# GLA and SSD of a hybrid mixer in three passes each: contributions, a walk over the states, outputs

## The chip, the cores and the metric

The kernel runs on one core of one Trainium2 chip. The metric is device time in microseconds for one execution of the whole program; where several runs are shown, it is their median. A time from the trace comes from one profiled execution.

## The reference

The program computes two layers of a mixer with four branches that share one input projection: RWKV-7, S5, SSD and GLA. A sequence has 256 context tokens and 1024 tokens of a grid, so 1280 columns in all; the model width is 1024 and each branch has 256 channels. Context and grid are separate sequences: the grid starts from the context's final state, and each branch runs in both directions. Layer 0 needs outputs of all 1280 tokens, layer 1 only of the 1024 (of the context it needs the states alone).

The two branches that matter here are chunked linear attentions. With d for the decay of a chunk, each keeps a state S for every head:

```
def chunk_state_pass(decay, contrib, s0):
    def step(S, inp):
        dec, ctb = inp
        return dec * S + ctb, S
    s_fin, prev = lax.scan(step, s0, (moveaxis(decay, 1, 0), moveaxis(contrib, 1, 0)))
    return moveaxis(prev, 0, 1), s_fin
# GLA: chunks of 64 tokens, 4 heads, 32 keys and 64 values a head, a decay for each key
contrib = einsum('bcqhk,bcqhv->bchkv', k * exp(b_last - bc), v)
y = einsum('bchij,bcjhv->bcihv', scores, v) + einsum('bcihk,bchkv->bcihv', q * exp(bc), prev)
# SSD: chunks of 128 tokens, 4 heads in 2 groups, 64 states, a decay for each head
contrib = einsum('bcqhn,bcqhp->bchnp', k * exp(cs_last - cs)[..., None], v)
y = einsum('bchij,bcjhp->bcihp', scores, v) + einsum('bcihn,bchnp->bcihp', q * exp(cs)[..., None], prev)
```

The outputs of both directions are added; then come a norm, a gate and, at the end of the layer, the output projection over all four branches.

## The kernel before

The program goes through each layer in three stages: the projection stage (`project`), the RWKV and S5 stage (`rw`) and the output projection (`out_proj`). GLA and SSD belong to the projection stage. Inside it the program order is: the projections of `misc` and `gk`, the preparation of S5, GLA with its projections, SSD with its projections, then the projections of RWKV and the rest. The framework schedules the instructions of all engines by a list: it takes program order as priority and a model of durations, so work that stands early in the program goes ahead where it is ready, and projections fill the rest of PE. The order of each engine is fixed at build time; on the chip each engine takes its queue in order and waits on semaphores.

Projections (`proj`, `proj_tok`, the tile `pj` in PSUM) multiply a split of each weight, `i_wh` and `i_wl`, made by ACT (L1550) and VectorE (L1551) from a load `i_w`, with a split of the normed input, `hi` and `lo`. Their results go through DRAM. All matmuls of the helper `mm` carry L320, all two-input elementwise operations L332, all activations L329, so the tiles tell them apart.

**GLA** (`gla`, L389). `qe` and `ke` are the scaled queries and keys of the two directions, features on the partitions (four heads of 32). The loop of L451 has 20 steps; a step handles one chunk of 64 forward and one backward (`ch`). In every second step two 128-column pieces of `ke` are transposed (`g_kp`), and in the first half of the loop `gla_pair` (L513) is called for the pair of chunks `j`: masked queries `g_qb`, scores in PSUM, mask (`g_P`), sum of both directions (`g_pa`), four matmuls with the values `V` (tile `l_gv`), and an ACT copy into `g_Y`. From step 1 on, two matmuls of 256 columns multiply `qe` by the state `g_S` (L472), and two VectorE operations add the result to `g_Y` (L476). Then eight small matmuls give the contributions of the step (L483), and VectorE adds them to the running state `g_Sd` (L488), spreads it over four heads by a mask into `g_S` (L491) and multiplies by the decay (L493). In layer 1 the outputs of the first four steps are left out.

**SSD** (`ssd`, L538). After a convolution (`s_cv`) and transposes (`s_xt`, `s_Bt`), the loop of L610 has 10 steps, one chunk of 128 forward and one backward. `ssd_pair` (L664) makes the part inside a chunk. The output term multiplies C (`s_x`) by the state `s_S` (L618), scales on VectorE (`s_yt`, L623) and adds on POOL (L625). Contributions come from weighted values `s_xw` made on POOL (L632) and matmuls with `s_Bt` (L635); VectorE updates the state `s_Sc` (L643, L644); ACT copies it into `s_S` (L648), whose zero blocks keep the groups apart.

Both end with a norm and a gate and with `y_out` (L374), which transposes the result on PE (L381, `ps<-con,s_Y`), scales on ACT and stores to DRAM. The large SBUF tiles of the stage (`T`) share eight buffers, the 2 KB tiles (`Q`) eleven. PSUM has the tags `pc` (2 buffers: states and contributions), `ps` (3), `pz` (1) and `pj` (2).

The RWKV stage starts with memsets, loads `r_in` and prepares its first blocks (`ps<-r_in`, a scan `r_cs`, `r_BK`, `r_AD`); its first large matmul is `pb<-r_AD,r_BK`.

Of the kernel before, what the change touches and what calls it, by code (L numbers as in the profile page):

```python
# [15 lines left out]
OP = mybir.AluOpType  # L16
# [238 lines left out]
class K:  # L255
# [133 lines left out]
    def gla(self, src, outs):  # L389
# [20 lines left out]
        gall, gs = self.S("gall", [128, 2, 20, 4]), self.S("g_gs", [128, 2, 20])  # L410
        k, q = src["gk"], src["gq"]
        for d in range(2):
# [19 lines left out]
            if d == 0:  # L432
                self.tt(g[:, 0:19], l3[:, 0:19], em[:, 1:20], OP.mult)
                nc.vector.tensor_copy(g[:, 19:20], l3[:, 19:20])
            else:
                self.tt(g[:, 0:3], l3[:, 3:0:-1], em[:, 2::-1], OP.mult)
                self.tt(g[:, 3:4], l3[:, 0:1], em[:, 19:20], OP.mult)
                self.tt(g[:, 4:19], l3[:, 19:4:-1], em[:, 18:3:-1], OP.mult)
                nc.vector.tensor_copy(g[:, 19:20], l3[:, 4:5])
            self.tt(gall[:, d], g.unsqueeze(2).to_broadcast([128, 20, 4]),  # L440
                    c("bm4").unsqueeze(1).to_broadcast([128, 20, 4]), OP.mult)
# [7 lines left out]
        Y = [self.T("g_Y", [128, 5, 256]) for _ in range(2)]  # L449
        St = Sp = None  # L450
        for s in range(20):  # L451
            ch = [s, 3 - s if s < 4 else 23 - s]
            jb = [x // 2 for x in ch]
            if s % 2 == 0:

                kp = next(kring)
                ps = self.P()
                for d in range(2):
                    nc.tensor.transpose(ps[:, d * 128:(d + 1) * 128], ke[d][:, jb[d] * 128:(jb[d] + 1) * 128], c("ident"))
                p3 = ps[:, :256].rearrange("p (a b) -> p a b", a=2)  # L460
                nc.scalar.copy(kp[0:64, :, 0, :], p3[0:64])
                nc.vector.tensor_copy(kp[64:128, :, 1, :], p3[64:128])
                first = s == 0 if s < 4 else s < 12
                if first and (outs or s >= 4):
                    for j in (jb if jb[0] != jb[1] else jb[:1]):
                        self.gla_pair(j, qe, ke, next(pring), V, Y)
            if s > 0 and (outs or s >= 4):

                ps = self.P("pc")[:, :256]
                for d in range(2):  # L470
                    r = 64 * (ch[d] % 2)
                    self.mm(ps[r:r + 64], qe[d][:, ch[d] * 64:(ch[d] + 1) * 64], St[:, d, :])  # L472
                for d in range(2):
                    j, r = jb[d], 64 * (ch[d] % 2)
                    y = Y[j // 5][r:r + 64, j % 5, :]
                    self.tt(y, ps[r:r + 64], y, OP.add)  # L476
            if s == 19:
                break
            ps = self.P("pc")[:, :128]
            for d in range(2):  # L480
                j, r = jb[d], ch[d] % 2
                for h in range(4):
                    self.mm(ps[32 * h:32 * h + 32, d * 64:(d + 1) * 64], kp[:, d, r, 32 * h:32 * h + 32], V[j // 5][:, j % 5, h * 64:(h + 1) * 64])  # L483

            cur = ps.rearrange("p (d v) -> p d v", d=2)
            Sd = self.S("g_Sd", [128, 2, 64], bufs=2)
            if Sp is not None:
                self.tt(Sd, cur, Sp, OP.add)  # L488
                cur = Sd
            Sn = self.Q("g_S", [128, 2, 256])  # L490
            self.tt(Sn.rearrange("p d (h v) -> p d h v", h=4), cur.unsqueeze(2).to_broadcast([128, 2, 4, 64]),  # L491
                    gall[:, :, s, :].unsqueeze(3).to_broadcast([128, 2, 4, 64]), OP.mult)
            self.tt(Sd, cur, gs[:, :, s:s + 1].to_broadcast([128, 2, 64]), OP.mult)  # L493
            Sp = Sd
            St = Sn
# [17 lines left out]
    def gla_pair(self, j, qe, ke, pa, V, Y):  # L513

        nc, c = self.nc, self.c
        pm = []
        halves = [slice(0, 64), slice(64, 128)]
        for d in range(2):
            qb = self.Q("g_qb", [128, 4, 128])
            self.tt(qb, qe[d][:, j * 128:(j + 1) * 128].unsqueeze(1).to_broadcast([128, 4, 128]),  # L520
                    c("bm4").unsqueeze(2).to_broadcast([128, 4, 128]), OP.mult, "p")
            ps = self.P()[:, :256]
            for h in halves:
                self.mm(ps[h], ke[d][:, j * 128 + h.start:j * 128 + h.stop], qb[:, :, h])
# [7 lines left out]
        ps = self.P()  # L532
        for h in range(4):
            self.mm(ps[:, h * 64:(h + 1) * 64], pa[:, h, :], V[j // 5][:, j % 5, h * 64:(h + 1) * 64])
        nc.scalar.copy(Y[j // 5][:, j % 5, :], ps[:, :256])  # L535


    def ssd(self, src, outs):  # L538
# [60 lines left out]
        Y = [self.T("s_Y", [128, 5, 256]) for _ in range(2)]  # L599
        cring = self.ring("s_cp", [128, 2, 128], 2)  # L600
        sring = self.ring("s_S", [128, 2, 256], 2)
# [7 lines left out]
        St = Sp = None  # L609
        for s in range(10):  # L610
            tl = [s, 1 - s if s < 2 else 11 - s]
            if (s == 0 or 2 <= s < 6) and (outs or s >= 2):
                for j in tl:
                    self.ssd_pair(j, B, C, next(cring), xt, stri, lap, dt, Y)
            if s > 0 and (outs or s >= 2):
                ps = self.P("pc")
                for d in range(2):
# [1201 lines left out]
```

## Time and profile before

| | us |
|---|---|
| median of 3 runs | 2274.1 |
| lowest and highest | 2272.3, 2274.61 |
| the profiled execution | 2271.75 |
| its span, first to last instruction | 2269.9 |

| engine | busy us | share of the span |
|---|---|---|
| PE (matmul) | 1970.1 | 87% |
| PEld (weight load) | 1652.5 | 73% |
| VectorE (DVE) | 1571.7 | 69% |
| ACT | 922.1 | 41% |
| POOL | 834.8 | 37% |

Busy shares are averages over the stages. By the stretches in which they run, the projection stage lies at about 0 to 669 us (layer 0) and 1290 to 1733 us (layer 1), the RWKV stage after each, the output projection last. PE's busy time counts matmuls from start to their modelled end; overlapping ones are counted once. The granted clock is the share of TensorE's full rate in a stretch. The waits of an engine name what ended an idle time.

### The profile page before, as it was taken

How to read it: one execution, taken by the hardware profiler on the slowest of the kernel's cores; microseconds unless marked ns; L12 is line 12 of the kernel's file. 1: busy time of each engine (PE TensorE's matmuls, PEld its weight loads, DVE VectorE, ACT ScalarE, POOL GpSimd, SP SyncE). 2: the span in 40 equal slices, each digit the busy share in tenths (PEclk: the TensorE clock that was granted, in tenths of full speed). 3: DMA queues.
4: the chain of work that ended last, by engine and by line, in shares of the span. 5: the costliest groups of instructions: out<-in, count | busy, mean ns of one | idle time of the engine just before them, and what ended most of it. 6: DMA issues, size and time to landing. Idle time of an engine off the chain costs nothing. (4 is left out here: it accounts for less than half of the span.)

```text
span 2269.9 us, 44142 instructions
## 1 busy us (share of the span) xinstructions
PE 1970.1 (87%) x17173; PEld 1652.5 (73%) x17176; DVE 1571.7 (69%) x3513; ACT 922.1 (41%) x2005; POOL 834.8 (37%) x947
## 2 busy tenths in 40 slices
PE   7797999999985888888998989999996678787897
PEld 5677788777774777766997777877885567676697
DVE  3876535866638987887477887368563898778654
ACT  3335212244436547544233552123452655564420
POOL 1446431113345535442322266301234355444222
PEclk9899999999997888898999899999998778797998
DMA  8134413454342323214333254234222232220532
GB/s 272 53 117 154 136 58 124 137 180 126 113 130 98 97 68 102 78 36 152 116 108 121 92 175 137 71 105 131 82 75 83 96 94 78 76 71 29 174 110 94
DMA packets 208049, 246.76 MB, mean 109 GB/s; under 512 B 28384, under 2 KB 150240, under 8 KB 207840
## 3 DMA queue, kind: packets, MB, share of 16 engines
q1 hardware_dynamic: 174832, 215.49, 30.4%
q10 hardware_dynamic: 33008, 28.45, 3.8%
q8 instruction: 135, 2.21, 0.4%
q14 instruction: 74, 0.61, 0.1%
HBM read 169.27 MB, written 76.71 MB: 108 GB/s over the span
## 5 line engine op out<-in xcount | busy, mean ns | idle before, releaser
L320 PE MATMUL pj<-hi,i_wh 128*128 128x512 f32 (+1 forms) x952 | 248.4, 381 | 19.2 <-DVE hi L1527 10.8
L320 PE MATMUL pj<-hi,i_wl 128*128 128x512 f32 (+1 forms) x952 | 247.4, 373 | 0.3 <-DVE i_wl L332 0.3
L320 PE MATMUL pj<-lo,i_wh 128*128 128x512 f32 (+1 forms) x952 | 245.9, 375 | 0.0
L320 PEld LDWEIGHTS pj<-hi,i_wh 128*128 128x128 f32 x952 | 169.4, 196 | 54.9 <-DVE hi L1527 11.3
L320 PEld LDWEIGHTS pj<-lo,i_wh 128*128 128x128 f32 x952 | 170.1, 195 | 35.1 <-issue 4.6
L320 PEld LDWEIGHTS pj<-hi,i_wl 128*128 128x128 f32 x952 | 166.6, 192 | 34.4 <-issue 5.0
L332 DVE TENSOR_TENSOR i_wl<-i_w,i_wh 128x512 fp32r<-128x512 f32 x108 | 86.3, 807 | 70.2 <-ACT i_wh L1550 34.4
L1550 ACT CAST i_wh<-i_w 128x512 fp32r<-128x512 f32 x108 | 66.3, 620 | 162.8 <-PE pj L320 127.3
L320 PE MATMUL pb<-r_AD,r_BK 128*128 128x256 f32 x320 | 98.3, 457 | 33.3 <-DVE r_BK L332 14.9
L320 PE MATMUL px<-r_UV,r_A 128*64 128x64 f32 x1216 | 109.4, 248 | 18.8 <-DVE r_UV L1378 9.5
L320 PEld LDWEIGHTS px<-r_UV,r_A 128*64 128x64 f32 x1216 | 93.5, 158 | 41.3 <-DVE r_UV L1378 13.5
L320 PEld LDWEIGHTS pb<-r_AD,r_BK 128*128 128x128 f32 x320 | 70.1, 231 | 47.8 <-POOL r_BK L332 22.8
L1288 DVE TENSOR_TENSOR r_X<-r_X,r_tp 128x30 f32<-128x30 f32 (+1 forms) x300 | 93.2, 311 | 7.7
L332 DVE TENSOR_TENSOR r_tp<-r_N,r_X 128x30 f32<-128x30 f32 (+1 forms) x300 | 91.4, 305 | 7.1
L332 DVE TENSOR_TENSOR g_Y<-pc,g_Y 64x256 f32<-64x256 f32 x70 | 29.4, 421 | 77.1 <-ACT g_Y L535 56.2
L332 POOL TENSOR_TENSOR r_S<-r_S,r_PM 64x256 f32<-64x256 f32 x72 | 54.7, 760 | 72.0 <-DVE r_S L332 66.8
L320 PE MATMUL pj<-i_wh,hi 128*128 128x256 f32 x448 | 71.6, 297 | 9.9 <-ACT i_o L329 5.0
L335 POOL TENSOR_SCALAR r_AD<-r_AR 64x512 f32<-64x512 f32 (+1 forms) x80 | 54.7, 684 | 50.9 <-PE pb L320 34.7
L320 PEld LDWEIGHTS pj<-i_wh,hi 128*128 128x128 f32 x448 | 61.9, 199 | 14.2 <-ACT i_wh L1550 5.6
L329 ACT ACTIVATE r_BK<-r_BK,r_PM 128x128 f32<-128x128 f32 x160 | 58.2, 399 | 31.7 <-PE pb L320 30.6
L332 POOL TENSOR_TENSOR s_Y<-s_Y,s_yt 128x256 f32<-128x256 f32 x34 | 29.1, 868 | 111.0 <-DVE s_Y L332 62.3
L320 PE MATMUL ps<-r_in,rconm 128*128 128x128 f32 x320 | 52.2, 312 | 19.5 <-ACT r_yt L1421 7.7
(466 smaller groups left out, 5156.1 us busy)
## 6 DMA issues: line engine op xcount, KB each, us to landing
i_w<-in_win SPq DMA_DIRECT2D x108, 256.0 KB, 3.0
r_in<-rm SPq DMA_DIRECT2D x36, 512.0 KB, 4.2
a_w<-in_ada SPq DMA_DIRECT2D x64, 256.0 KB, 3.2
rm<-i_o SPq DMA_DIRECT2D x48, 256.0 KB, 2.7
o_y<-yd SPq DMA_DIRECT2D x36, 256.0 KB, 3.2
i_o<-in_ada SPq DMA_DIRECT2D x32, 256.0 KB, 5.2
z_st<-s5t SPq DMA_DIRECT2D x32, 256.0 KB, 2.8
o_w<-in_wout SPq DMA_DIRECT2D x32, 256.0 KB, 2.9
```

Of the source, the lines that this page charges most:

```text
L320: self.nc.tensor.matmul(out, lhsT, rhs, start=start, stop=stop, skip_group_check=True)
L329: self.nc.scalar.activation(out=out, in_=in_, func=f, **kw)
L332: (self.nc.vector if e == "v" else self.nc.gpsimd).tensor_tensor(out, a, b, op)
L335: (self.nc.vector if e == "v" else self.nc.gpsimd).tensor_scalar(out, a, s1, s2, op0, op1)
L1288: last = nc.vector.tensor_tensor(X[:, :, :i, r0:4], X[:, :, :i, r0:4], tmp[:, :, :i, r0:], OP.add)
L1550: self.nc.scalar.copy(hi[:, v], w)
```

## The change

GLA: the loop of 20 steps becomes three passes. The first goes over the ten pieces of 128 columns: transposes, `g_kp`, sixteen small matmuls for the contributions of both chunks and directions into one PSUM tile, and two copies (VectorE for the forward, ACT for the backward direction) into the SBUF tiles `g_St`, ordered by step. The second is a walk over the 19 states in place: add the state before, multiply by the decay. The third calls `gla_pair` for each pair; it now adds the output of the states into the same PSUM bank as the part inside the chunk, by up to sixteen matmuls that take the masked queries `g_qb` as weights and 64 columns of a state. One ACT copy then writes the result over the values `V`. The spreading of the state over heads, its mask `gall`, `g_S` and the VectorE additions into `g_Y` are gone.

SSD: contributions of all ten chunks first, with copies into `s_St`; a walk of eight steps on VectorE (multiply, add); then for each chunk `ssd_pair` and the output term, whose matmuls now take the masked C (`s_cp`) of one group and 128 columns of a state, two for each direction. Both directions are scaled by one VectorE operation where both exist. The result overwrites the values `s_xt`.

```
@@ gla
-        Y = [self.T("g_Y", [128, 5, 256]) for _ in range(2)]
-        St = Sp = None
-        for s in range(20):
-            ...
+        St = [self.T("g_St", [128, 10, 2, 64]) for _ in range(2)]
+        step = lambda d, ch: ch if d == 0 else 3 - ch if ch < 4 else 23 - ch
+        for j in range(10):
+            ps = self.P()[:, :256]
             for d in range(2):
+                nc.tensor.transpose(ps[:, d * 128:(d + 1) * 128], ke[d][:, j * 128:(j + 1) * 128], c("ident"))
+            kp = next(kring)
+            ...
+            ps = self.P("pc")[:, :256].rearrange("p (d r v) -> p d r v", d=2, r=2)
+            for d in range(2):
                 for h in range(4):
-                    self.mm(ps[32 * h:32 * h + 32, d * 64:(d + 1) * 64], kp[:, d, r, 32 * h:32 * h + 32], V[j // 5][:, j % 5, h * 64:(h + 1) * 64])
-            ...
+                    for r in range(2):
+                        self.mm(ps[32 * h:32 * h + 32, d, r], kp[:, d, r, 32 * h:32 * h + 32], V[j // 5][:, j % 5, h * 64:(h + 1) * 64])
+            for d in range(2):
+                a = step(d, 2 * j)
+                ...
+                (nc.scalar.copy if d else nc.vector.tensor_copy)(o, ps[:, d])
+        for t in range(19):
+            o = St[t // 10][:, t % 10]
+            if t:
+                self.tt(o, o, St[(t - 1) // 10][:, (t - 1) % 10], OP.add)
+            self.tt(o, o, gs[:, :, t:t + 1].to_broadcast([128, 2, 64]), OP.mult)
+        Y = V
+        for j in range(0 if outs else 2, 10):
+            self.gla_pair(j, qe, ke, next(pring), Y, St, step)
@@ gla_pair
-        ps = self.P()
+        ps = self.P("pc")
+        y = Y[j // 5][:, j % 5]
         for h in range(4):
-            self.mm(ps[:, h * 64:(h + 1) * 64], pa[:, h, :], V[j // 5][:, j % 5, h * 64:(h + 1) * 64])
-        nc.scalar.copy(Y[j // 5][:, j % 5, :], ps[:, :256])
+            self.mm(ps[:, h * 64:(h + 1) * 64], pa[:, h, :], y[:, h * 64:(h + 1) * 64], h == 0, False)
+        for d in range(2):
+            for r in range(2):
+                ch = 2 * j + r
+                t = step(d, ch) - 1
+                if t >= 0:
+                    for h in range(4):
+                        self.mm(ps[64 * r:64 * r + 64, h * 64:(h + 1) * 64], qb[d][:, h, 64 * r:64 * r + 64], St[t // 10][:, t % 10, d], False, d == 1)
+        nc.scalar.copy(y, ps[:, :256])
@@ ssd
-        Y = [self.T("s_Y", [128, 5, 256]) for _ in range(2)]
+        Y = xt
-        sring = self.ring("s_S", [128, 2, 256], 2)
-        St = Sp = None
-        for s in range(10):
-            ...
+        St = [self.T("s_St", [128, 5, 2, 2, 64]) for _ in range(2)]
+        for j in range(10):
             ps = self.P("pc")
             xw = self.Q("s_xw", [128, 2, 4, 64])
             ...
+            for d in range(2):
+                t = step(d, j)
+                (nc.scalar.copy if d else nc.vector.tensor_copy)(St[t // 5][:, t % 5, d].rearrange("p h v -> p (h v)"), ps[:, d * 128:(d + 1) * 128])
+        for t in range(1, 9):
+            o, i = [St[u // 5][:, u % 5] for u in (t, t - 1)]
+            m = self.S("s_Sm", [128, 2, 2, 64], bufs=2)
+            self.tt(m, i, dc[:, :, t].unsqueeze(3).to_broadcast([128, 2, 2, 64]), OP.mult)
+            self.tt(o, o, m, OP.add)
+        for j in jobs:
+            cp = next(cring)
+            self.ssd_pair(j, B, C, cp, xt, stri, lap, dt, Y)
+            ds = [d for d in range(2) if step(d, j) > 0]
+            ps = self.P("pc")
+            for d in ds:
+                for g in range(2):
+                    self.mm(ps[:, d * 256 + g * 128:d * 256 + g * 128 + 128], cp[:, g], St[(step(d, j) - 1) // 5][:, (step(d, j) - 1) % 5, d].rearrange("p h v -> p (h v)"))
+            yt = self.Q("s_yt", [128, 2, 4, 64])
+            ...
```

## Rows read from the trace of the kernel before

**Rows 1.** Stretches: length, busy PE, PEld, DVE, ACT, POOL (count), PE clock, DMA.

```profile
250.00:418.00 168.00, 167.09 (x1381) 131.99 (x1380) 82.98 (x211) 33.54 (x67) 39.62 (x55) 0.99 0.33 104
...
519.00:655.00 136.00, 136.00 (x917) 104.59 (x916) 77.74 (x161) 53.18 (x123) 43.26 (x54) 1.00 0.37 110
...
669.50:686.70 17.20, 5.63 (x46) 5.02 (x45) 9.31 (x16) 10.59 (x22) 10.97 (x19) 0.80 0.86 279
1366.00:1530.00 164.00, 157.55 (x1232) 123.91 (x1230) 97.82 (x223) 37.07 (x77) 53.76 (x62) 0.97 0.32 101
...
1605.00:1733.50 128.50, 128.50 (x682) 105.52 (x682) 70.48 (x140) 54.58 (x123) 41.29 (x48) 1.00 0.24 69
1733.50:1768.20 34.70, 11.21 (x60) 9.51 (x61) 19.43 (x36) 11.96 (x26) 19.96 (x25) 0.62 0.36 109
```

**Rows 2.** Timeline of PE, end of layer 0's projections: start, length, operation, count [idle].

```profile
667.50 1.10 PE L320 MATMUL pj<-lo,i_wh 128*128 128x512 f32 x4
668.43 1.09 PE L320 MATMUL pj<-hi,i_wl 128*128 128x512 f32 x4
670.29 0.77 PE L381 MATMUL ps<-con,s_Y 128*128 128x128 f32 x5 [0.77 <-DVE s_Y L332]
...
686.66 3.73 PE L320 MATMUL pb<-r_AD,r_BK 128*128 128x256 f32 x8 [7.80 <-DVE r_BK L332]
```

**Rows 3.** Timeline of PE, end of layer 1's projections.

```profile
1732.39 1.10 PE L320 MATMUL pj<-hi,i_wl 128*128 128x512 f32 x4
1733.42 0.66 PE L320 MATMUL pc<-s_xw,s_Bt 128*64 128x128 f32 x8
...
1760.90 0.87 PE L381 MATMUL ps<-con,s_Y 128*128 128x128 f32 x3 [17.95 <-DVE qst L338]
...
1768.24 2.19 PE L320 MATMUL pb<-r_AD,r_BK 128*128 128x256 f32 x8
```

**Rows 4.** Timelines of DVE and POOL in the same place.

```profile
1736.76 0.76 DVE L332 TENSOR_TENSOR s_yt<-pc,s_ex 128x256 f32<-128x256 f32 x2 [2.21 <-PE pc L320]
...
1751.14 3.74 POOL L332 TENSOR_TENSOR s_sq<-s_Y 128x768 f32<-128x768 f32 x2
...
1762.27 1.49 DVE L332 TENSOR_TENSOR s_Y<-s_Y,qsy 128x1280 f32<-128x1280 f32 x1
```

**Rows 5.** Groups over the whole span: operation, count | busy us, mean ns | idle before.

```profile
L320 PE MATMUL px<-r_UV,r_A 128*64 128x64 f32 x1216 | 109.4, 248 | 18.8 <-DVE r_UV L1378 9.5 <-ACT r_UV L1347 7.7 <-POOL r_UV L1348 1.1
...
L320 PE MATMUL ps<-r_in,rconm 128*128 128x128 f32 x320 | 52.2, 312 | 19.5 <-ACT r_yt L1421 7.7 <-ACT r_a L329 6.9 <-DVE r_yt L338 4.8
...
L332 DVE TENSOR_TENSOR g_Y<-pc,g_Y 64x256 f32<-64x256 f32 x70 | 29.4, 421 | 77.1 <-ACT g_Y L535 56.2 <-PE pc L320 19.9
...
L332 DVE TENSOR_TENSOR g_S<-g_Sd,gall 128x512 f32<-128x512 f32 x36 | 28.9, 804 | 1.2
...
L320 PE MATMUL pc<-g_S,g_e 128*64 128x256 f32 x140 | 24.7, 410 | 0.7 <-DVE g_S L332 0.7
...
L320 PE MATMUL pc<-l_gv,g_kp 128*32 128x64 f32 x608 | 19.4, 228 | 0.4 <-DVE g_Y L332 0.4
...
L320 PE MATMUL pc<-s_S,s_x 128*128 128x256 f32 x68 | 18.8, 387 | 1.4 <-ACT s_S L648 1.4
...
L320 PE MATMUL pc<-s_xw,s_Bt 128*64 128x128 f32 x144 | 13.6, 290 | 0.0
```

**Rows 6.** Timeline of PE: one run of narrow RWKV matmuls and what follows.

```profile
1812.00 2.08 PE L320 MATMUL px<-r_UV,r_A 128*64 128x64 f32 x32
1814.01 0.75 PE L320 MATMUL pi<-r_DN,r_Am 32*32 32x32 f32 x64
```

**Rows 7.** Waits of PE from 1340 to 1734 us: total, times, longest.

```profile
PE pj L320 <- DVE i_o L338: 5.3, 8, 1.4
```

**Rows 8.** Timelines of SP and DVE where layer 1's GLA loop ends.

```profile
1529.52 0.33 SPq L1639 DMA_DIRECT2D l_sB<-f_sB  x1
...
1529.97 0.42 DVE L332 TENSOR_TENSOR g_Y<-pc,g_Y 64x256 f32<-64x256 f32 x1
```

## What the change will do, predicted before its result was known

> **What bounds the kernel now.** I read the busy time by stretch first, then the projection stage of each layer alone, then the two places where that stage hands over to the RWKV stage. GLA and SSD run inside the projection stage, beside the big projection matmuls, so the question is which engine is never free there. In the stretch of the GLA loop of layer 0 PE is busy 167.09 of 168 us, VectorE 82.98 and ACT 33.54; in the stretch of the SSD loop PE is busy 136.00 of 136; in layer 1 it is 157.55 of 164 and 128.50 of 128.5, at a granted clock of 0.97 to 1.00, that is the 2.4 GHz level nearly throughout [rows 1]. So while projections are left, PE work is the time, and VectorE has half of its time free: what the change saves on VectorE is worth little there by itself.
>
> Then come the two hand-overs. In layer 0 the last projection matmuls start at 668.43, the first big RWKV matmul (pb) at 686.66 [rows 2]; of that stretch of 17.2 us PE works 5.63 [rows 1]. In layer 1 the last projections start at 1732.39, but pb only at 1768.24 [rows 3]: 34.7 us with 11.21 busy, and the clock falls to 0.62 [rows 1]. The difference is the SSD of layer 1: its last output term (s_yt) is made at 1736.76, after the last projection; POOL squares at 1751.14; VectorE scales the result at 1762.27 [rows 4]; and PE, which takes its queue in order, stands 17.95 us before the transposes of s_Y at 1760.90 with pb queued behind them [rows 3]. In layer 0 the same transposes cost it 0.77 us [rows 2].
>
> **The change part by part.** Its time is counted against the profiled execution: 2271.75 us, 1.85 above its span of 2269.9; the median of the three runs, 2274.1, lies 2.35 higher, and I carry the difference over to the median.
>
> 1. GLA outputs on PE. Before, each step multiplies qe by the state St, spread to four heads: two matmuls of 64 output rows by 256 columns. A float32 matmul stands in the trace as two instructions, so the 19 + 16 steps make the 140 of the group, busy 24.7 us, 176 ns each [rows 5]. Now each pair of chunks makes up to sixteen matmuls of 64 columns, one for each direction, chunk and head: 152 in layer 0, 128 in layer 1, so 560 instructions. The nearest row is the RWKV matmul with the same shapes (128x64 weights, 64 columns): over the whole kernel 109.4 us for 1216, 90 ns each with all ends [rows 5]; in one unbroken run 32 of them take from 1812.00 to 1814.01, 63 ns each [rows 6]. A pair's sixteen are such a run of 32, so I take 63: 35.2 us, 10.5 more than now. The upper end is 90 ns: 50.4, 25.7 more. The lower end is below nothing: the present pairs lie in different halves of the output rows, and that two column groups can overlap is seen at the contributions, 608 instructions in 19.4 us or 32 ns each [rows 5]; if the two halves overlapped fully in the new order too, 35.2 would become 17.6, 7.1 less than now.
>
> Here a rule of the Trainium skill speaks against part of my price. The rows show 63 ns for narrow matmuls that follow one another in one half, and 32 ns where four column groups take turns [rows 5, 6]. The Trainium skill, "TensorE: Matmul & The Clock Gate", section "Part 3: Packing small matmuls — row/col tiling", says that matmuls in different column groups run at once but start strictly in program order. The new order does four in one half before the other half, so by that rule only the last of each four overlaps with its successor. What it would make is a rival below.
>
> 2. GLA contributions: 152 matmuls a layer become 160 (both directions of all ten pairs), 608 instructions become 640. At the present 32 ns that is 1.0 us more [rows 5], and I take it. The order is new: two chunks of one head, in one group of 32 rows, before the next head. The lower end is 0; the upper end, with no overlap left at all, is 63 ns, 20.9 more.
>
> 3. SSD outputs: 34 matmuls of 256 columns (68 instructions, 18.8 us) become 68 of 128 columns. The nearest row is the 128x128 by 128 matmul of the RWKV inputs, 52.2 us for 320 or 163 ns [rows 5]: 136 of these are 22.2, 3.4 more, which I take. Ends: 0 if it goes by columns alone, 18.7 if each costs 276 ns as the wide ones do.
>
> 4. SSD contributions: 36 a layer become 40, at 13.6 us for 144 instructions [rows 5]: 1.5 more.
>
> 5. Turns of PE. Four projection matmuls take 0.93 us when the next ones follow (667.50 to 668.43) and 1.03 when GLA or SSD work follows (1732.39 to 1733.42) [rows 2, 3]: a turn costs 0.1. GLA turned for 19 + 16 outputs and 38 contributions; it now turns 20 times for contributions, and the outputs go with the pair's last matmuls. 53 turns fewer are 5.3 us; many already shared a visit, so I take 3 (ends 0 and 5.3).
>
> PE's sum: 10.5 + 1.0 + 3.4 + 1.5 - 3 = 13.4 us more, and since PE is full it lies on the path.
>
> 6. VectorE, ACT and POOL. Gone are the spreading of the state to four heads (28.9 us) and the additions into g_Y (29.4) [rows 5], with ACT's copies of the SSD state; new are 40 copies of contributions out of PSUM on each of VectorE and ACT; the walk has as many small operations as the loop had. Some 45 us of VectorE are saved, all under PE's cover: I count the work at nothing. If that cover were gone it would be worth at most what PE now loses to VectorE there: the projections' waits for i_o are 5.3 us in layer 1 [rows 7]. I take 2 back. Either way is possible, since the convolution of SSD moves up beside those i_o operations, and i_o and the weight splits are queued behind each VectorE wait of the new pass: 5 gained to 5 lost.
>
> 7. Chains. In the GLA of before, output, addition and state share two PSUM buffers with the contributions of the next steps; the loop takes 164 us in layer 1 [rows 1]. SSD's loads start when it ends: sB is fetched at 1529.52 as the last g_Y is added at 1529.97 [rows 8]. In SSD each step goes PE, VectorE, ACT, PE, and each PE visit stands behind projections, so it ends at 1736.76 [rows 4]. Now both walks stay on VectorE, and the outputs of different pairs don't depend on each other. The added waits are: the walk for the last contribution, all outputs for the walk, and SSD's x times D on POOL for the four matmuls that read x (it now overwrites it; POOL's s_sg of the next pair is queued behind). None is for PE's projections. SSD need end only some 35 us earlier than now for its transposes, and the POOL and VectorE work before them, to lie under projections. Then the hand-over of layer 1 is like that of layer 0: 34.7 - 17.2 = 17.5 us less [rows 1]. What comes last then is the RWKV preparation itself (r_in, its scan, r_BK), which layer 0 shows. In layer 0 the 0.77 us go [rows 2]; I count 1 (0 to 3). No DMA is added; loads of SSD and the final stores move to earlier, where SP and ACT's queue have room.
>
> The sum: 13.4 - 17.5 - 1 - 2 = -7.1 us: 2264.6 for the profiled execution, **2267 us** for the median.
>
> **The rivals.** (a) The order rule above: of each four matmuls three run alone and the fourth beside the next, so 27.5 us instead of 35.2 (estimate from the 63 ns), PE +5.7 and the sum -14.8: 2259. For it speaks that one-group runs and taking turns differ in the rows as it says. Chance 0.20. (b) Both halves overlap fully, since the four instructions of a GLA step do so now: outputs -7.1, PE -4.2, sum -24.7: 2249. Against it: half of the order is in one group. Chance 0.13. (c) Slower: narrow matmuls cost 90 ns because sixteen in a row don't hide their weight loads, in both GLA loops, where nothing covers PE: PE +28.6, sum +8.1: 2282. It decides from 75 ns an instruction on, where the outputs' 42 us eat all that the hand-over gives. Against it: the unbroken run at 63. Chance 0.12. (d) Slower too: the hand-over stays, because all pairs of SSD are now queued after its walk and the last still ends after the last projection: 13.4 - 2 = +11.4: 2285. For it: pairs use the same three PSUM buffers as before; against it: the serial steps are gone from both loops. Chance 0.12.
>
> **How the numbers follow.** The forecast's own case has 0.35, from 2258 to 2275; 0.08 is left for shifts of order that I can't place, both ways. A measurement of this kernel tells about 0.2%, 4.5 us, from no change: faster is below 2269.6, slower above 2278.6. Faster: 0.23 of the forecast's case, all of (a) and (b), 0.02: 0.58. Slower: (d), 0.08 of (c), which reaches below the bound, and 0.03 of the rest: 0.23. Same: 0.12 of the forecast's case, 0.04 of (c) and 0.03 of the rest: 0.19. The range goes from 2242, below (b), to 2288, above (d). All upper ends of 1 to 3 at once would be 2315; I give that less than 0.05 and leave it out.
>
> **What would show it.** Right: the g_St matmuls at about 63 ns in runs of 32, some 35 us in all; the projections of layer 1 ending 5 to 10 us later after the stage's start than now; s_Y's transposes ahead of the last projections; pb within 18 us of them in both layers; PE still full between. Wrong: idle time of PE beside the walk; s_Y's transposes still last in layer 1; a price of narrow matmuls far from 63 ns; or a projection stage whose length doesn't follow PE's sum.

## The result: 30 us less, with the profile after

The changed kernel takes **2244.4 us** (median of four runs, 2239.62 to 2248.43) against 2274.36 us (four runs, 2272.3 to 2277.87) for the kernel before: ratio 0.9866, 95% interval 0.9843 to 0.9889. The profiled execution takes 2239.62 us with a span of 2237.8, 32.1 us under the 2269.9 of before. It was forecast to be faster, at 2267 within 2242 to 2288; the gain is four times the forecast one. The profiled execution is the quickest of the four. One of the six executions of rotate_c below took 5761 us and is left out of its median.

The two traces are cut at the same landmarks: first and last projection matmul of a layer, first big RWKV matmul (pb), first output projection. So the stretches are, in order: projection stage, hand-over and RWKV stage of layer 0; output projection of layer 0 with the projection stage of layer 1, hand-over and RWKV stage of layer 1; output projection at the end. Columns as in [rows 1]. The kernel before:

```profile
core 0: us, PE busy (x) PEld busy (x) DVE busy (x) ACT busy (x) POOL busy (x), PEclk, DMA share, GB/s
5.28:668.43 663.15, 609.98 (x4447) 487.96 (x4449) 401.32 (x871) 223.23 (x454) 218.99 (x212) 0.96 0.41 130
668.43:686.66 18.23, 6.66 (x50) 5.55 (x48) 10.38 (x20) 10.59 (x22) 11.78 (x19) 0.82 0.87 286
686.66:1080.43 393.77, 322.59 (x3810) 267.50 (x3810) 326.31 (x735) 210.51 (x507) 179.03 (x238) 0.85 0.29 88
1080.43:1732.39 651.96, 608.08 (x4252) 523.64 (x4251) 437.02 (x997) 235.72 (x463) 204.06 (x195) 0.96 0.34 108
1732.39:1768.24 35.85, 12.37 (x65) 10.20 (x64) 19.76 (x37) 11.96 (x26) 21.00 (x26) 0.63 0.35 106
1768.24:2147.25 379.01, 303.17 (x3687) 253.47 (x3688) 311.24 (x696) 203.37 (x489) 169.38 (x231) 0.85 0.27 85
2147.25:2269.90 122.65, 107.26 (x868) 104.16 (x868) 65.37 (x157) 23.70 (x41) 30.32 (x23) 0.92 0.35 111
```

The changed kernel:

```profile
5.30:663.80 658.50, 608.01 (x4758) 497.82 (x4759) 385.27 (x832) 216.94 (x458) 217.45 (x212) 0.96 0.43 134
663.80:679.52 15.72, 5.11 (x33) 4.14 (x32) 6.32 (x8) 7.20 (x16) 12.08 (x19) 0.76 0.69 239
679.52:1072.60 393.08, 313.60 (x3797) 259.00 (x3797) 327.45 (x724) 211.05 (x507) 176.36 (x238) 0.87 0.28 85
1072.60:1723.99 651.39, 612.40 (x4538) 539.97 (x4537) 428.86 (x996) 231.69 (x467) 213.06 (x204) 0.96 0.35 109
1723.99:1743.74 19.75, 8.51 (x35) 7.04 (x34) 4.77 (x7) 7.25 (x17) 9.91 (x17) 0.66 0.77 242
1743.74:2117.12 373.38, 297.30 (x3689) 249.22 (x3689) 317.68 (x709) 207.59 (x498) 173.67 (x231) 0.87 0.27 86
2117.12:2237.80 120.68, 105.61 (x869) 102.98 (x868) 57.23 (x143) 20.16 (x35) 29.42 (x23) 0.94 0.33 102
```

Row by row, after minus before: the two projection stages -4.7 and -0.6, the hand-overs -2.5 and -16.1, the RWKV stages -0.7 and -5.6, the end -2.0. They add up to the 32.1, and 18.6 of it are the hand-overs. PE is busy in the projection stages for 1220.4 us in place of 1218.1: the 13.4 us more that the forecast charged to PE are not there. VectorE's busy time in them falls from 838.3 to 814.1, and the stages don't follow it.

The hand-over of layer 1, timeline of PE in the changed kernel (it answers to [rows 3]):

```profile
1665.24 1.14 PE L381 MATMUL ps<-con,s_xt 128*128 128x128 f32 x9
...
1723.99 1.10 PE L320 MATMUL pj<-hi,i_wl 128*128 128x512 f32 x4
1729.74 1.66 PE L320 MATMUL ps<-r_in,rconm 128*128 128x128 f32 x8 [4.65 <-DMA r_in<-rm]
...
1743.74 2.47 PE L320 MATMUL pb<-r_AD,r_BK 128*128 128x256 f32 x5 [4.13 <-DVE r_BK L332]
```

The transposes of SSD's result (now held in s_xt) start at 1665.24, between projections and 59 us ahead of the last of them; the wait of 17.95 us is gone. What comes last between the last projection and pb is RWKV's own preparation: its load, and then r_BK.

PE's groups, whole span (they answer to [rows 5]):

```profile
L320 PE MATMUL pc<-g_St,g_qb 128*64 128x64 f32 x560 | 28.0, 228 | 0.4 <-DVE g_St L332 0.4
L320 PE MATMUL pc<-s_St,s_cp 128*128 128x128 f32 x136 | 20.0, 279 | 0.0
L320 PE MATMUL pc<-s_xw,s_Bt 128*64 128x128 f32 x160 | 14.1, 285 | 0.0
L320 PE MATMUL pc<-l_gv,g_kp 128*32 128x64 f32 x640 | 13.5, 223 | 0.0
```

GLA's outputs cost 28.0 us (24.7 before), its contributions 13.5 (19.4), SSD's outputs 20.0 (18.8), its contributions 14.1 (13.6).

### The profile page after: what moved, and what is told of

Same layout as the page of the kernel before. It is cut to its first block, busy times and chain, and to the rows that moved or that the text cites. A ratio compares the mean times of both kernels' runs of the same rounds, so it can differ in the third digit from the quotient of the medians.

```text
span 2237.8 us, 45114 instructions
## 1 busy us (share of the span) xinstructions
PE 1950.5 (87%) x17712; PEld 1660.2 (74%) x17712; DVE 1528.0 (68%) x3423; ACT 904.9 (40%) x2001; POOL 832.2 (37%) x947
## 5 line engine op out<-in xcount | busy, mean ns | idle before, releaser
L320 PE MATMUL pj<-hi,i_wh 128*128 128x512 f32 (+1 forms) x952 | 247.2, 379 | 15.3 <-DVE hi L1512 11.1
L320 PE MATMUL pj<-hi,i_wl 128*128 128x512 f32 (+1 forms) x952 | 241.4, 370 | 2.5 <-DVE i_wl L332 2.5
L320 PEld LDWEIGHTS pj<-hi,i_wh 128*128 128x128 f32 x952 | 169.6, 197 | 50.9 <-DVE hi L1512 11.5
L320 PE MATMUL px<-r_UV,r_A 128*64 128x64 f32 x1216 | 108.8, 248 | 14.1 <-DVE r_UV L1363 8.2
L320 PEld LDWEIGHTS ps<-r_in,rconm 128*128 128x128 f32 x320 | 48.8, 227 | 28.2 <-ACT r_yt L1406 10.2
L320 PE MATMUL pu<-r_rs,r_TT 128*64 128x128 f32 x320 | 48.8, 301 | 22.5 <-ACT r_rs L1359 22.4
```

Of the source, the lines that this page charges most:

```text
L320: self.nc.tensor.matmul(out, lhsT, rhs, start=start, stop=stop, skip_group_check=True)
```

## Experiments

Theory A, formed on these traces: the gain has three sources. SSD's tail comes under the projections because GLA's step-by-step loop no longer holds SSD back; PE's new small matmuls cost no more than the old ones, by their order; and the RWKV stages, whose code is untouched, got shorter by an order that came out differently. The rivals are named in the expectations. Each run has its own runs of the kernel before on the same chip beside it; ratios are against those.

**One part of the change alone.** GLA in three passes with SSD as before, and the other way round.

```diff
 gla_only
     gla, gla_pair: as changed
-    ssd: as changed
+    ssd: as before
 ssd_only
-    gla, gla_pair: as changed
+    gla, gla_pair: as before
     ssd: as changed
```

> GLA in three passes, SSD as in the kernel before. Theory A (SSD came late because GLA's step-by-step loop came before it): GLA ends some 67 us sooner in layer 1, SSD's last output term falls under the projections, so the hand-over of layer 1 falls from 35.8 us (last projection to first pb) to about 20, the projection stages lose about 3 to 5 us, and the time is 20 to 26 us under that of before, about 2250. Theory B (SSD's own reshaping shortens the hand-over): hand-over stays at 30 or more, time 2262 to 2272.

> SSD in three passes, GLA as in the kernel before. Theory A: GLA's loop still ends near 1529 in layer 1, and SSD needs about 200 us from there to its transposes in the changed kernel, so these come at about 1735, at the end of the projections: part of the hand-over is saved, 5 to 14 us, time 2258 to 2270. Theory B: hand-over of layer 1 at 20, time 2250 to 2258.

Measured: GLA alone 2251.07 us, ratio 0.9919 (0.9906 to 0.9932); SSD alone 2262.91 us, ratio 0.9971 (0.9959 to 0.9983). The hand-over of layer 1 in the one and in the other, and the projection stages of SSD alone, as rows of stretches:

```profile
1732.18:1751.22 19.04, 8.66 (x36) 6.93 (x34) 4.77 (x7) 7.25 (x17) 9.90 (x17) 0.65 0.80 251
```

```profile
5.38:671.56 666.18, 611.86 (x4511) 490.78 (x4513) 409.65 (x883) 218.55 (x450) 217.86 (x212) 0.95 0.42 133
1086.50:1747.05 660.55, 613.98 (x4308) 532.84 (x4306) 444.90 (x1014) 237.70 (x461) 210.92 (x202) 0.95 0.34 106
1747.05:1766.64 19.59, 10.21 (x49) 7.65 (x49) 13.56 (x20) 10.74 (x24) 12.50 (x19) 0.72 0.68 210
```

Either part alone brings the hand-over to 19 to 20 us. With GLA alone the hand-over is as theory A has it, and the time nearly (18.9 us under the kernel before beside it, 20 to 26 expected); the projection stages did not get the 3 to 5 us shorter that I had expected. With SSD alone the transposes do come late, as expected, but cost nothing more. Timeline of PE there:

```profile
1748.83 1.16 PE L320 MATMUL ps<-r_in,rconm 128*128 128x128 f32 x8 [0.24 <-ACT i_o L329]
...
1758.72 2.18 PE L381 MATMUL ps<-con,s_xt 128*128 128x128 f32 x9 [3.95 <-DVE s_xt L332]
...
1766.64 1.65 PE L320 MATMUL pb<-r_AD,r_BK 128*128 128x256 f32 x3
```

They start at 1758.72, 11.7 us after the last projection, beside the preparation, which needs till 1766.64 anyway. So the hand-over has slack; I had expected 5 to 14 us saved, and 16 were: the hand-over of theory B with the time of theory A. The gains of the parts don't add, since both remove the same wait: 16.8 and 16.3 us in the hand-over of layer 1, against 16.1 together. The rest of the difference lies in the projection stages: 1315.1 us before, 1316.1 with GLA alone, 1326.7 with SSD alone, 1309.9 with both. Why SSD alone makes them longer by 11.6 is not shown; what the timelines tell is that PE leaves the projections 195 times for other work there, 180 times with GLA alone and 168 with both (counted from 200 to 700 and from 1300 to 1770 us). The turns alone don't explain it, since the kernel before leaves them 214 times in stages of 1315.1 us.

**Is PE's work the time in the projection stage?** The changed kernel without the 560 matmul instructions on GLA's states.

```diff
-        for d in range(2):
-            for r in range(2):
-                ch = 2 * j + r
-                t = step(d, ch) - 1
-                ...
```

> The changed kernel without the 560 matmul instructions that multiply queries with the states of GLA (its outputs then lack the part from earlier chunks). If PE work in the projection stage is the time there, both layers together lose about 28 us (some 14 each) and the stage ends by so much sooner, time about 2216. If something else paces the stage (VectorE's split of the weights, loads), less than 14 us are lost in all.

Measured: 2236.16 us, ratio 0.9855 (0.9841 to 0.9869). The projection stages:

```profile
5.35:657.32 651.97, 601.52 (x4453) 487.27 (x4455) 390.59 (x832) 217.61 (x458) 218.28 (x212) 0.96 0.43 136
1077.94:1721.99 644.05, 603.00 (x4273) 527.88 (x4274) 429.94 (x984) 231.37 (x467) 213.36 (x204) 0.96 0.35 110
```

The stages give back 13.9 us (1309.9 to 1296.0), half of the 28 expected, and by the number alone just on the side of the other theory; two profiles of one program differ by up to 6.4 us in this sum (below), so the number alone doesn't decide. The mechanism of the other theory is not there: PE's busy time falls by 15.9 and its idle time stays (89.5 and 91.5), so no other engine paces the stage. Wrong was to take the group's 28.0 us for what it adds. A group's busy time holds ends that overlap with what follows; and without the outputs PE leaves the projections 186 times in place of 168, and the projections' own matmuls take 6 us more (937.2 to 943.2, summed over their groups). In the total even less is left, since the RWKV stages came out 7.4 us longer (773.9 against 766.5).

**The order of GLA's outputs.** One run of 32 instructions, with the neighbours in the two halves of the output rows changing 3 times (the changed kernel), 15 times, or once.

```diff
 alt_halves, outputs
-        for d in range(2):
-            for r in range(2):
-                    for h in range(4):
+        for d in range(2):
+            for h in range(4):
+                for r in range(2):
 same_half, outputs
+        for r in range(2):
+            for h in range(4):
+                for d in range(2):
```

> The changed kernel, with GLA's output matmuls of one direction alternating between the two halves of the output rows (head outside, chunk inside) instead of four in one half and then four in the other. If only neighbours in different column groups overlap, the 560 instructions go from 28.0 us (50 ns) to about 18 (32 ns), and the time falls by about 10 us against the changed kernel. If matmuls into one bank of PSUM do not overlap at all, or the order does not matter, 28 to 35 us and no difference.

> The changed kernel with all matmuls of one half of the output rows before the other half (chunk outside, then head, then direction): one change of half in a run of 32 instructions, where the changed kernel has three and the alternating version fifteen. From the runs of 1.47 and 1.08 us, an instruction that follows one in its own half costs 51 ns and one that changes half 18 ns, so 31 instructions follow at 30 x 51 + 18: 1.55 us, and the group is about 29 us; at the 63 ns of the prediction it would be 35. The compiled order of TensorE in layer 0's RWKV stage is the same here as in the changed kernel, in layer 1 it differs: by theory C (the order of the stage sets its length) layer 0's RWKV stage is 390 to 396 again, against 408 to 410 with alternating halves; by theory D it may lie anywhere from 390 to 410.

Timelines of PE, one run and what follows it: the changed kernel, alternating halves, one half first.

```profile
282.15 1.54 PE L320 MATMUL pc<-g_St,g_qb 128*64 128x64 f32 x32
283.62 1.10 PE L320 MATMUL pc<-l_gv,g_pa 128*128 128x64 f32 x8
```

```profile
282.83 1.15 PE L320 MATMUL pc<-g_St,g_qb 128*64 128x64 f32 x32
283.91 1.10 PE L320 MATMUL pc<-l_gv,g_pa 128*128 128x64 f32 x8
```

```profile
294.47 1.90 PE L320 MATMUL pc<-g_St,g_qb 128*64 128x64 f32 x32
296.30 1.10 PE L320 MATMUL pc<-l_gv,g_pa 128*128 128x64 f32 x8
```

From start to next start: 1.47, 1.08 and 1.83 us, or 46, 34 and 57 ns an instruction; as groups 28.0, 21.1 and 33.9 us. The order sets the price. My two-price sum for one half first (29 us) was wrong, the 63 ns of the forecast (35) nearly right: going from one change to three saves 0.36 us, from three to fifteen only 0.39 more. The times: alternating halves **2257.56 us**, ratio 0.9950 (0.9935 to 0.9965); one half first 2251.78, ratio 0.9921 (0.9900 to 0.9942). The version with the cheapest outputs is slower than the changed kernel, though its projection stages are 2.7 us shorter (1307.2). The stretches say where: its RWKV stage of layer 0.

**Does an RWKV stage's length belong to the kernel or to the execution?** The changed kernel and the alternating one once more.

> The changed kernel once more, beside the next three on one chip. In the first profiles its two RWKV stages (first pb to first out-projection) summed to 766.5 us, those of the kernel before to 772.8, those of the version with alternating halves to 788.5. Theory C (the length of these stages belongs to a kernel, by its order of instructions there): the sum is 762 to 771 again. Theory D (it belongs to the execution, by the granted clock it happens to get): it can lie anywhere from 760 to 790. Time 2240 to 2248 by C.

> Alternating halves once more. Theory C: RWKV stages sum to 783 to 793 again and the time is 10 to 16 us above that of the changed kernel in this call, though its projection stages are some 3 us shorter. Theory D: the difference to the changed kernel goes, and the time is 0 to 7 us below it.

Measured: the changed kernel 2242.43 us, ratio 0.9875 (0.9855 to 0.9894); alternating halves 2261.82, ratio 0.9958 (0.9943 to 0.9973). RWKV stage of layer 0 in the second profile of the changed kernel, in both of the alternating one, and with one half first:

```profile
679.40:1071.63 392.23, 313.63 (x3796) 258.46 (x3796) 326.37 (x724) 211.50 (x507) 176.17 (x238) 0.87 0.28 85
```

```profile
678.73:1088.79 410.06, 330.01 (x3820) 273.19 (x3821) 330.57 (x738) 212.82 (x507) 175.65 (x238) 0.81 0.27 85
```

```profile
682.36:1090.75 408.39, 324.10 (x3821) 267.96 (x3821) 329.90 (x738) 212.72 (x507) 176.76 (x238) 0.83 0.27 85
```

```profile
683.03:1075.22 392.19, 315.16 (x3796) 259.97 (x3796) 325.76 (x724) 211.41 (x507) 175.70 (x238) 0.87 0.28 85
```

The alternating version is 19.4 us above the changed kernel, more than theory C had it (10 to 16), and theory D is out. Theory C holds in layer 0: 393.1 and 392.2 for the changed kernel, 410.1 and 408.4 for the alternating one, and 392.2 for the third kernel, in whose program PE's instructions of that stage stand in the same order as in the changed kernel (buffer numbers left out). In the alternating one they don't: of its 390 rows of instructions there some 60% match. The stage's code is the same in all, and the order of its instructions is made anew for each program; an edit of three loops some hundred us earlier is enough to change it. The rows say what the other order costs: PE's idle time is 79.5 us in the changed kernel and 80.1 and 84.3 with alternating halves, but its busy time is 313.6 against 330.0 and 324.1 for nearly the same matmuls, at a granted clock of 0.87 against 0.81 and 0.83. With levels of 1.2 and 2.4 GHz, these means stand for some 102 us of the stage at the lower one in the changed kernel and for some 156 and 139 with alternating halves (estimates from the rows). So most of the 16 to 17 us are nearly the same matmuls at the lower clock level for more of the time.

**Both cheap orders, and more samples of the RWKV stage.** GLA's contributions with neighbours in four column groups, as in the kernel before, with three orders of the outputs.

```diff
 alt_crot, rotate_c, both_fast: contributions
-                for h in range(4):
-                    for r in range(2):
+                for r in range(2):
+                    for h in range(4):
 outputs, outer to inner: alt_crot d, h, r; rotate_c r, d, h; both_fast h, d, r
```

> Alternating halves, and GLA's contributions in the order of the kernel before too (chunk outside, head inside, so that neighbours lie in four different column groups). If overlap goes by the neighbour's column group, the 640 contribution instructions cost less than the 13.5 us of the changed kernel, about 9 to 11; if the fall from 19.4 us came from the longer runs (32 instructions in place of 16 a visit) alone, they stay at 13 to 14. The projection stages end 0 to 4 us sooner than with alternating halves alone. On the RWKV stages: by theory C a sum of its own, by D anything.

> GLA's contributions with neighbours in four column groups (as in the kernel before), and outputs with one half before the other (chunk, direction, head). Contributions 11 to 12 us in place of 13.5, outputs about 29. TensorE's compiled order in layer 1's RWKV stage is that of the changed kernel, in layer 0 it is far from it: by theory C layer 1's RWKV stage is 371 to 379 and layer 0's has a length of its own.

> Both cheap orders: outputs alternate halves (head, direction, chunk) and contributions rotate over the four column groups. Outputs 21 us, contributions 11 to 12, projection stages together 1305 to 1310 (1309.9 in the changed kernel). Its order in both RWKV stages is its own; if their sum is 765 as in the changed kernel, the time is 2238 to 2242, and if it is 772 to 788, 2245 to 2262: the 8 us saved on TensorE's small matmuls then show only where that order allows it.

Groups of alt_crot, rotate_c and both_fast:

```profile
L320 PE MATMUL pc<-l_gv,g_kp 128*32 128x64 f32 x640 | 11.6, 226 | 0.0
```

```profile
L320 PE MATMUL pc<-g_St,g_qb 128*64 128x64 f32 x560 | 33.7, 225 | 0.0
L320 PE MATMUL pc<-l_gv,g_kp 128*32 128x64 f32 x640 | 11.0, 221 | 0.0
```

```profile
L320 PE MATMUL pc<-g_St,g_qb 128*64 128x64 f32 x560 | 21.2, 226 | 0.8 <-DVE g_St L332 0.8
L320 PE MATMUL pc<-l_gv,g_kp 128*32 128x64 f32 x640 | 11.8, 230 | 0.0
```

The contributions' fall from 19.4 us has two parts. In the old order they cost 11.0 to 11.8 in the new structure, 17 to 18 ns each: that is the longer run (up to 64 instructions in a visit, 247.64 to 248.74 in the changed kernel, where a step had 16). The new order gives about 2 us of it back. Times and stages of all profiles; "stages" is the sum of the two projection stages, us:

| kernel | median | ratio (interval) | stages | RWKV 0 (clock) | RWKV 1 (clock) |
|---|---|---|---|---|---|
| before | 2274.36 | | 1315.1 | 393.8 (0.85) | 379.0 (0.85) |
| changed | 2244.4 | 0.9866 (0.9843-0.9889) | 1309.9 | 393.1 (0.87) | 373.4 (0.87) |
| changed, again | 2242.43 | 0.9875 (0.9855-0.9894) | 1310.0 | 392.2 (0.87) | 371.8 (0.85) |
| gla_only | 2251.07 | 0.9919 (0.9906-0.9932) | 1316.1 | 395.5 (0.86) | 375.6 (0.86) |
| ssd_only | 2262.91 | 0.9971 (0.9959-0.9983) | 1326.7 | 399.3 (0.85) | 371.5 (0.87) |
| alt_halves | 2257.56 | 0.9950 (0.9935-0.9965) | 1307.2 | 410.1 (0.81) | 378.5 (0.85) |
| alt_again | 2261.82 | 0.9958 (0.9943-0.9973) | 1313.6 | 408.4 (0.83) | 377.8 (0.85) |
| alt_crot | 2247.45 | 0.9896 (0.9876-0.9916) | 1307.2 | 404.9 (0.83) | 366.6 (0.86) |
| rotate_c | 2247.94 | 0.9908 (0.9886-0.9930) | 1322.2 | 385.5 (0.87) | 379.3 (0.84) |
| both_fast | 2256.14 | 0.9940 (0.9917-0.9964) | 1310.9 | 401.9 (0.84) | 373.3 (0.85) |
| no_gla_out | 2236.16 | 0.9855 (0.9841-0.9869) | 1296.0 | 404.9 (0.84) | 368.9 (0.86) |
| same_half | 2251.78 | 0.9921 (0.9900-0.9942) | 1320.4 | 392.2 (0.87) | 377.6 (0.86) |
| sep_bank | 2259.22 | 0.9937 (0.9920-0.9954) | 1325.3 | 391.8 (0.86) | 379.7 (0.85) |

The RWKV stage of layer 0 ranges over 385.5 to 410.1 us with the order it happens to get, that of layer 1 over 366.6 to 379.7; two profiles of one kernel differ by at most 1.7. In layer 1 PE's order alone does not settle it: the changed kernel, gla_only, alt_halves and rotate_c have the same one there and take 371.8 to 379.3. Which other engine's order does it, and why an order keeps the clock up, stays open. The two cheap orders together save 8.5 us of group time (41.5 to 33.0) and none in the end: none of the versions that compute everything beats the changed kernel. The projection stages of one program also differ between profiles, by 6.4 us in the alternating one (1307.2, 1313.6), so that differences of a few us in them are not evidence. The 5.2 us by which they got shorter under the change are such a difference; the 18.6 us of the hand-overs are not.

**The bank that adds up.** GLA's products with the states go to a second bank and VectorE adds them.

```diff
-            self.mm(..., pa[:, h, :], y[...], h == 0, False)
+            self.mm(..., pa[:, h, :], y[...])
+        nc.scalar.copy(y, ps[:, :256])
+        ps = self.P("pc")
         ...
-        nc.scalar.copy(y, ps[:, :256])
+        self.tt(y, ps[:, :256], y, OP.add)
```

> The changed kernel, but GLA's products with the states go to a second bank of PSUM and VectorE adds them to the copied output (18 additions more in all, some 0.6 us each). Prediction's step 6: VectorE has room under PE, so the projection stages change by less than 2 us in all. Rival: the bank that adds up is what shortens the stages, and they grow by 5 us or more.

Measured: 2259.22 us, ratio 0.9937 (0.9920 to 0.9954). Projection stages:

```profile
5.37:671.38 666.01, 614.21 (x4758) 500.45 (x4759) 392.33 (x842) 217.60 (x458) 217.51 (x212) 0.96 0.42 133
1078.93:1738.20 659.27, 617.05 (x4530) 542.90 (x4529) 430.85 (x992) 231.26 (x467) 209.54 (x204) 0.95 0.34 106
```

1325.3 us against 1310.0 in the changed kernel beside it, more than twice what two profiles of one program differ by. The time is as the rival has it; that the bank is the cause is not shown. One half first and rotate_c keep the one bank, and their stages are 10.4 and 12.3 us longer than in the changed kernel's first profile, with GLA's outputs and contributions only 6.4 and 3.2 dearer, so a new order alone can add several us. VectorE's own part is small (its busy time goes from 811.5 to 823.2, PE's idle time from 92.5 to 94.0). PE's busy time grows by 13.8 for the same matmul instructions: it leaves the projections 182 times in place of 168, and the same groups cost more, spread thinly over projections, SSD and GLA (PE's groups in the two stages together 1484.7 against 1468.0). I can't split that further with these runs.

## Why the prediction held in direction and missed the size

In us, against the profiled execution:

| step | forecast | measured |
|---|---|---|
| GLA outputs | +10.5 | +3.3 |
| GLA contributions | +1.0 | -5.9 |
| SSD outputs | +3.4 | +1.2 |
| SSD contributions | +1.5 | +0.5 |
| turns of PE | -3 | -9.3 in the projections' matmuls (cause not shown) |
| all of PE in the projection stages | +13.4 | -0.6 by groups, +2.3 busy |
| waits of PE there | -2 | -7.6 idle (-4.5 in the second profile) |
| hand-over, layer 1 | -17.5 | -16.1 |
| hand-over, layer 0 | -1 | -2.5 |
| RWKV stages and the end | 0 | -8.3 |
| sum | -7.1 | -32.1 |

**The hand-over was right**, in place, mechanism and size: SSD's tail moved under the projections, and layer 1's hand-over became like that of layer 0. Two of the signs named for it did not come: pb starts within 18 us in layer 0 (15.7) but narrowly not in layer 1 (19.8), and layer 1's projections end no later than before. The slower rival (d) fell, and the two part-alone runs show that it would have taken both loops as before to keep the wait.

**PE's sum was wrong by 14 us, in two terms above all.** For GLA's outputs I took the price of an unbroken run in one half. That price is real (57 ns with one half first), but the new order changes halves three times in a run, and it costs 46 ns in the run, 50 with the ends of the visits: 28.0 us, where rival (a) had 27.5. Rival (c)'s 90 ns and rival (b)'s full overlap (17.6 us) did not come; even fifteen changes leave 21.1. I had given rival (a) 0.20 and should have put it first, since the rows that I had read hold both of its prices.

The rule behind that rival is that of the Trainium skill, "TensorE: Matmul & The Clock Gate", section "Part 3: Packing small matmuls — row/col tiling": matmuls in different column groups run at once, but start in program order. The three runs agree with it in their order, 1.83, 1.47 and 1.08 us with one, three and fifteen changes of half, but not in size. As rival (a) used it, a change saves one matmul, that is two instructions of 63 ns or 0.126 us, and three changes in sixteen matmuls would make 28.6 us of the 35.2, not 27.5. Against the unbroken run of 2.01 us [rows 6] one change saves 0.18 us and three save 0.54, so some three instructions each. A timeline of PE in the changed kernel, where a run in the second half is followed by work in the first, shows the same reach:

```profile
284.66 1.37 PE L320 MATMUL pc<-g_St,g_qb 128*64 128x64 f32 x29
285.81 0.43 PE L320 MATMUL ps<-g_qb,g_s 128*64 128x256 f32 x1
285.86 0.34 PE L320 MATMUL pc<-g_St,g_qb 128*64 128x64 f32 x3
```

The first instruction of the next pair starts when 29 of the 32 have started, and the last three start after it. Whether PE's queue holds them in that order the traces don't tell, so the part of the rule on program order stays open. That 28.0 lies so near to 27.5 is in part luck: the 28.0 hold the ends of the visits, and the 46 ns of the runs alone make 25.7.

For GLA's contributions I took 32 ns from [rows 5] as a price per instruction. It held the ends of 38 short visits of 16; in runs of up to 64 the same instructions cost 17 to 21 ns. The lower bound of that term should have been below nothing.

**Turns.** 46 fewer by the timelines (214 to 168), where I had counted 53, and the projections' own matmuls take 9.3 us less (946.5 to 937.2), which would be 0.2 us for each turn where I took 0.1 from two rows. That it is the turns is not shown. The run with two banks points that way, 14 turns more and the stage longer; but SSD alone has 19 turns fewer than the kernel before, and its projection matmuls take 947.4 us; and two profiles of one program differ by 2.5 (937.2 and 934.7) and 3.4 us (938.9 and 942.3) in this sum. Part of it is given back, because 5.0 us of SSD's transposes now lie in the stage: the other groups grow by 9.6 in all.

**Waits.** PE's idle time in the projection stages fell from 97.1 to 89.5 us (92.5 in the second profile of the changed kernel). Waits of PE in layer 0's stage, before and after:

```profile
PE pj L320 <- DMA i_o<-in_ada: 13.7, 7, 5.3
PE pj L320 <- DVE i_o L338: 3.9, 4, 2.2
```

```profile
PE pj L320 <- DMA i_o<-in_ada: 5.3, 4, 1.7
PE pj L320 <- ACT a_c L329: 5.3, 1, 5.3
PE pj L320 <- DVE i_o L338: 0.2, 1, 0.2
```

The loads are those of the kernel's start, ahead of the change, and they fell by 3.1 us, to 10.6, and not by 8.4: the wait of 5.3 us at the very start, put down to the load before, is put down to ACT's a_c after. The second profile has 11.1 for the loads. VectorE's i_o fell by 3.7 us, to 0.2 in both profiles, and stays at 4.1 with SSD alone, so that part comes with GLA's three passes. It is the 2 us that step 6 of the forecast took back, in the other layer: in layer 1's stretch of [rows 7], where I looked, i_o costs PE 5.9 us as against 5.3. Counted from the 701st projection matmul of each layer to the 2201st and the 1901st, which leaves the starts out, the stages took 418.1 and 338.2 us before and 420.1 and 335.1 after: -1.1 together, where PE's groups say -0.6 for the whole stages. Both lie within what two profiles of one program differ by. So nothing speaks against "the stage follows PE's sum"; the sum was wrong.

**The RWKV stages** were counted at nothing, as code that the change doesn't touch. They and the end gave 8.3 us here and 11.5 in the second profile (772.8 + 122.7 before, 764.1 + 119.9). That their length belongs to the order which comes out of a kernel is shown for layer 0 by the repeats and by the third kernel of the same order; for layer 1, which holds 5.6 of the 8.3, and for the end it is not shown. It is luck as far as the change goes: alternating halves, with the same code in these stages, got 788.5 where the changed kernel got 766.5. Rival (b), 2249, is nearest to the result by its number, for a reason that did not occur. Without the RWKV stages and the end the profiled time would have fallen by 23.8 us, near rival (b)'s 24.7 only by chance.

## What to carry to other kernels

Before pricing a small matmul, look at what its neighbours are: the same 560 instructions cost 34, 28 or 21 us by the order of three loops, and a price from short visits holds their ends and is too high for long runs. A group's busy time is not what its removal gives (28 us listed, 14 gained in one profile of each). Where a program's order is made anew with each edit, an untouched stage can move by 10 us or more, so a change worth 1% is judged by stretches between landmarks and by a second variant, and not by the total alone.

## What the runs showed that I had not expected

Nearly the same matmuls in the same stage took 313.6 or 330.0 us of busy time by order alone, at granted clocks of 0.87 and 0.81; with PE's order unchanged layer 0's stage came out within 0.9 us (392.2 to 393.1) in three profiles of two kernels. The hand-over between stages has slack of its own: with SSD alone changed its transposes began 11.7 us after the last projection and cost nothing, because the next stage's preparation took 19.6 us anyway.
